# Output stage of a hybrid step: one half of the prompt tile moved behind the last pair, loads in a fixed order, and conversions tied behind gates

## The chip, the cores and the metric

The kernel runs on one core of a Trainium2 chip. The metric is the device time of one execution in microseconds, as the median of several runs. The engines of the core work from separate instruction lists, each in its own order: PE multiplies matrices into PSUM banks, ACT (ScalarE), DVE (VectorE) and POOL (GpSimd) work element by element, and SP (SyncE) issues most of the DMAs. POOL and ACT issue the others.

## The reference

One layer is computed for 128 prompt tokens and 2048 sample tokens of width 1024. A modulated RMSNorm is followed by one wide input projection; three branches (a gated delta rule, a spatial gating unit and a Fourier mixing) each give 512 columns. What matters here is the end:

```python
pb = jnp.einsum('btnw,nwd->btnd', br, w_branch)
gt = jax.nn.sigmoid(gates.reshape(B, T, N_BRANCH, D_MODEL))
merged = jnp.einsum('btnd,btnd->btd', gt, pb)
return jnp.einsum('btd,de->bte', merged, w_out), s_f, s_b
...
h = h + gate * out
y_prompt = rmsnorm(h, final_g)
```

The same last two lines, with the other group's gate, give `y_sample`.

## The kernel before

**Operands.** Each float32 operand of a product is split into a scaled float16 high part and low part, and a product is three matmuls (high by high, high by low, low by high). Weights are split on the chip: `converting` (line 289) squares a loaded block on ACT (line 305) to find its size, works out a power of two, and then writes the high part on ACT (line 317) and the low part on DVE (line 318). The loaded block waits in one of two buffers `wst`.

**Merges.** `merge` (line 1683) runs once for each branch, in the order 1, 2, 0. For each of eight blocks of output columns (`db`) and each of five token groups (four of 512 tokens, one of the 128 prompt tokens) it runs one unit: a projection of the normalized tokens `xh`, `xl` for the gate (24 matmuls), its sigmoid on ACT into `sg` (line 1714), a projection of the branch's output `o16` (12 matmuls; tile name `big`), the product of both on DVE (line 1723) and the running sum on POOL (line 1724). Both projections take their PSUM bank from a pool of three (`ps_mm`); the gate's bank is free once the sigmoid has read it. While one branch's last column block runs, `branch_block` (line 1672) loads the next branch's output into `st` and splits it into `o16` (lines 1678 and 1679). In the last merge (branch 0) the token groups run in the order 1024, 1536, prompt, 0, 512, and from column block 4 on `quarters` (line 1851) takes the finished block and the one four before it, makes the seven operand sums of a Strassen product in `T7` (two buffers), splits them (`as_pair`, lines 1809 and 1810) and writes them to the DRAM tile `pa` by a DMA that POOL issues (line 1865).

**Output.** The output projection is done in pairs of token tiles: `two_tiles` (line 1987) makes a 256-token by 1024 result from seven products of 12 matmuls of 512 columns, 84 in place of 96. The stationary operand comes from `pa` (one load of 1792 KB for a pair), the moving one from the split output weights `wohi`, `wolo`, or from sums of their quarters, which lie in DRAM as `tw` and are loaded once (four loads of 1024 KB, line 1941). The gate vector is multiplied in, the row of x added, and the row normalized (`rows_done`, line 1952). The prompt's tile is done apart and in full, by `one_tile` (line 1959): two halves of 24 matmuls, with the operands `p16` that the last merge left. Before the change it runs first, ahead of the eight pairs `firsts = [8, 10, 12, 14, 0, 2, 4, 6]`. The last pair ends by pieces, so that little is left after its last matmul: its last product is cut into 384 and 128 columns.

**Space.** The rows of x and the results lie in `room`, which is the place of `xh`; `tw` lies in the place of `xl`. A load into such a place waits only for the matmuls that still read those bytes. The pool `opa`, with two buffers of pair operands, lies where `o16` was, so a load into it waits until the last matmul of the last merge. A third buffer lies in the pool `orp`.

**What sets the order.** The program is traced in the order of the source, and a planner then gives each engine its list: it plays the program against estimated costs and takes what is ready, by priority. `tc.high_priority()` raises the priority of a block. `with tc.issue_after(x)` forbids that an instruction in the block stands ahead of `x` in the list of the same engine; it adds no wait for x's result. `gated_[0]` is the newest sigmoid traced. Each engine runs its list strictly in order, so an instruction that waits holds up all that stand behind it. The DMAs that SP issues run through one queue.

Of the kernel before, what the change touches and what calls it, by code (L numbers as in the profile page):

```python
# [188 lines left out]
def hybrid_flow_kernel(ctx: ExitStack, tc: tile.TileContext, x_prompt, x_sample, state_delta, c, c_ctx, w_ada,  # L189
# [48 lines left out]
    newest = [None]  # L238
# [55 lines left out]
    def converting(w, st, nkt, cols=P, hi=None, lo=None, tag="w", bufs=5, nth=0):  # L294
# [10 lines left out]
        w.squared = A.activation(w.lo, st, AF.Square, accum_out=ss)  # L305
# [1366 lines left out]
    def branch_block(n, s, t0, tn):  # L1672

        for g in range(4):
            st = sb(ep, [P, tn], "st", bufs=3)
            SY.dma_start(st, obD[n][g, :, t0:t0 + tn])
            yield
            A.activation(o16[:, 0, g, t0:t0 + tn], st, AF.Copy, scale=s)  # L1678
            V.scalar_tensor_tensor(o16[:, 1, g, t0:t0 + tn], st, s, o16[:, 0, g, t0:t0 + tn], ALU.mult, ALU.subtract)  # L1679

    gated_ = [None]
# [126 lines left out]
    def as_pair(hi, lo, src, s):  # L1808
        A.activation(hi, src, AF.Copy, scale=s)
        V.scalar_tensor_tensor(lo, src, s, hi, ALU.mult, ALU.subtract)  # L1810

# [38 lines left out]
    def quarters(k, t0, m4, mr):  # L1850
# [10 lines left out]
        as_pair(T7[:, :, 0, 0], T7[:, :, 1, 0], x4[:, :, 0], ms_s)  # L1861
        as_pair(T7[:, :, 0, 1:3], T7[:, :, 1, 1:3], x8, ms_s)
# [22 lines left out]
    p16, gp = [], []  # L1885
# [7 lines left out]
    def ahead_out(h0):  # L1893
        if h0:
# [3 lines left out]
            for i in range(2):  # L1898
                gp.append(sb(ep, [P, 512], "sg", bufs=4))
                SY.dma_start(gp[i], gateD[1:2, i * 512:(i + 1) * 512].to_broadcast([P, 512]))  # L1900
                scale_gate(gp[i], gp[i], winv[:, 4 * i:4 * i + 4])
            gp.append(sb(wp, [P, D], "wst", bufs=2))
            SY.dma_start(gp[2], gateD[0:1, :].to_broadcast([P, D]))
            scale_gate(gp[2], gp[2], winv)
# [20 lines left out]
    opa = pool(ctx, "opa", 2)  # L1925
    op = pool(ctx, "op", 2)
    room = xh.rearrange("p k t -> p (k t)").bitcast(F32)
    tw = xl.rearrange("p k t -> p (k t)")[:, 0:16 * D].rearrange("p (q j l k c) -> p q j l k c", q=4, j=4, l=2, k=4)
    firsts = [8, 10, 12, 14, 0, 2, 4, 6]
    ready = []  # L1930
    gb, fg = gp[2], sb(op, [P, D], "fg", bufs=1)

    def next_pair():
        i = len(ready)
        if i < len(firsts):
            ready.append(operands(orp, 1) if i % 3 == 2 else operands(opa, 2))
            SY.dma_start(ready[i].rearrange("p k l n c -> p k (l n c)"), paD[firsts[i] // 2].rearrange("k p x -> p k x"))

    next_pair()
    for q in (1, 2, 0, 3):  # L1940
        SY.dma_start(tw[:, q].rearrange("p j l k c -> p j (l k c)"), tD[q])
    SY.dma_start(fg, final_g[None, :].to_broadcast([P, D]))
    nth = [0]

    def two_rows(t, n):
        nth[0] ^= 1
        xr, hh = [[room[:, (4 * i + 2 * nth[0] + j) * D:(4 * i + 2 * nth[0] + j + 1) * D] for j in range(2)] for i in range(2)]
        for j in range(n):
            SY.dma_start(xr[j], xrows((t + j) * P, P))
        return xr, hh  # L1950

    def rows_done(t, hh, xr):
# [4 lines left out]
        SY.dma_start(y_sample[0, t * P:(t + 1) * P] if t < 16 else y_prompt[0], hh)  # L1957

    def one_tile(t, prepared, xr, hh):
        mh, ml = prepared  # L1960
        for i in range(2):
            cs = slice(i * 512, (i + 1) * 512)
            ps = bank(ps_mm, [P, 512])
            gemm_N(ps, mh, ml, wo, i * 512, 512)
            with tc.high_priority():
                V.tensor_tensor(gp[i], ps, gp[i], ALU.mult)
            G.tensor_tensor(hh[:, cs], gp[i], xr[:, cs], ALU.add)
        rows_done(t, hh, xr)
# [12 lines left out]
    def summed(q):  # L1981
        return lambda l, k: tw[:, q, :, l, k, :]

    odd_pair = [0]

    def two_tiles(t, pa, xr, hh, end):
# [5 lines left out]
        left, right = slice(0, 512), slice(512, D)  # L1992
# [19 lines left out]
        (V if end else G).tensor_tensor(hh[0][:, left], hh[0][:, left], xr[0][:, left], ALU.add)  # L2012
# [15 lines left out]
        parts = [sb(op, [P, 3], f"part{j}", bufs=1) for j in range(2)]  # L2028
        hf = [room[:, (6 - 2 * nth[0] + j) * D:(7 - 2 * nth[0] + j) * D] for j in range(2)]

        def piece(j, i, cs, on):
# [81 lines left out]
```

## Time and profile before

| | us |
|---|---|
| median of 3 runs | 2173.16 |
| lowest and highest | 2171.73, 2174.27 |
| the profiled execution | 2164.11 |
| its span | 2162.3 |
| PE busy, of the span | 2083.1 |
| granted TensorE clock, mean over the span | 0.992 |

The profile is of one execution. Times in its views are microseconds from the start of the span. A row of the timeline gives start, duration, engine, line, operation, output and inputs, and in brackets the idle time before it with what ended that. The view by windows gives the busy time of each engine in a stretch, then the granted TensorE clock as a share of full speed, the share of the DMA engines in use and GB/s. `SPq` and `POOLq` are the sequencers that issue DMAs.

### The profile page before, as it was taken

Reading aid. Unit: us, or ns where it says so; the run is one execution under the profiler, and the core shown is the slowest. Engines: PE = TensorE matmul, PEld = TensorE weight load, DVE = VectorE, ACT = ScalarE, POOL = GpSimd, SP = SyncE. Lnnn points to the kernel's source line nnn. Section 1 sums busy time; section 2 is a strip of 40 time slices with the busy share of each in tenths; the row PEclk is TensorE's granted clock in tenths of the full one; section 3 lists DMA queues with packets and bytes.
Section 4 is the critical chain, followed back from the end, with each engine's and each line's share of the span. In section 5 each row is a group of like instructions: output and inputs, shape, how many; then the busy total and the mean of one; then the engine's idle time right before and its main releaser. Section 6 shows DMA issues by size and latency. Waiting matters only on the chain.

```text
span 2162.3 us, 42634 instructions
## 1 busy us (share of the span) xinstructions
PE 2083.1 (96%) x16121; PEld 1193.1 (55%) x16121; DVE 1371.2 (63%) x3100; ACT 1062.1 (49%) x2453; POOL 753.1 (35%) x933
## 2 busy tenths in 40 slices
PE   7999999999899999899899999999999999998997
PEld 4455444456455677787565565556555444444443
DVE  6656854389778797466655546766564565565345
ACT  5554744476555663445544446655553444443111
POOL 0321432233333332443322233345443243333454
PEclk9999999999999999999999999999999999999999
DMA  9526732277776743443755556867654554556652
GB/s 351 218 77 197 256 122 81 83 232 219 243 227 223 234 148 92 132 148 112 232 170 171 164 168 184 266 204 228 210 183 163 166 185 157 182 201 263 245 217 104
DMA packets 222766, 403.24 MB, mean 186 GB/s; under 512 B 39704, under 2 KB 109744, under 8 KB 219744
## 3 DMA queue, kind: packets, MB, share of 16 engines
q1 hardware_dynamic: 167520, 290.58, 42.2%
q0 software_dynamic: 15216, 65.89, 8.1%
q10 hardware_dynamic: 39824, 44.05, 6.1%
q8 instruction: 126, 2.06, 0.4%
q14 instruction: 80, 0.66, 0.1%
HBM read 258.19 MB, written 142.24 MB: 185 GB/s over the span
## 4 chain that ended last, share of the span: by engine, by line
PE 45%; DVE 7%; DMA 6%; issue 2%; ACT 2%; POOL 1%; SPq 0%; POOLq 0%; DVEq 0%; ACTq 0%
PE b L241 44%; DMA st<-br 2%; DMA pa<-pa 1%; DMA wst<-in_w_ada_dram 1%; DVE XB L1103 1%; DVE E L1104 1%; DMA ei<-XB 1%; DVE big L1679 0%; DVE wlo L318 0%; DMA N<-n 0%; ACT big L1678 0%; POOL o L1359 0%; DVE S L1332 0%; DVE sg L466 0%; DVE o L1237 0%
## 5 line engine op out<-in xcount | busy, mean ns | idle before, releaser
L241 PE MATMUL b<-xh,whi 128*128 128x512 f16 (+1 forms) x1920 | 649.7, 347 | 3.3 <-DVE sg L1443 2.4
L241 PE MATMUL b<-xl,whi 128*128 128x512 f16 (+1 forms) x1920 | 649.9, 347 | 0.0
L241 PE MATMUL b<-xh,wlo 128*128 128x512 f16 (+1 forms) x1920 | 649.0, 347 | 0.0
L241 PEld LDWEIGHTS <-whi 128*128 128x128 f16 x3872 | 352.5, 98 | 327.6 <-issue 13.1
L241 PEld LDWEIGHTS <-wlo 128*128 128x128 f16 x1936 | 189.5, 98 | 177.6 <-issue 2.4
L241 PE MATMUL b<-big,bhi 128*128 128x512 f16 (+1 forms) x960 | 252.4, 348 | 5.0 <-ACT sg L1714 3.0
L241 PE MATMUL b<-big,blo 128*128 128x512 f16 (+1 forms) x480 | 163.6, 348 | 0.0
L1724 POOL TENSOR_TENSOR mrow<-mrow,sg 128x512 f32<-128x512 f32 (+1 forms) x80 | 93.1, 1168 | 149.1 <-DVE sg L1723 94.2
L241 PEld LDWEIGHTS <-xh 128*128 128x128 f16 x1496 | 117.2, 98 | 31.9 <-DVE yT L1629 2.6
L241 PEld LDWEIGHTS <-bhi 128*128 128x128 f16 x960 | 87.3, 98 | 78.0 <-issue 4.1
L943 POOL TENSOR_TENSOR cy<-cy,raw 128x545 f32<-128x545 f32 (+1 forms) x48 | 66.3, 1409 | 182.7 <-ACT raw L942 182.7
L1714 ACT ACTIVATE sg<-b,winv 128x512 f32<-128x512 f32 (+1 forms) x120 | 73.9, 616 | 96.0 <-PE b L241 95.2
L241 PEld LDWEIGHTS <-pa 128*128 128x128 f16 x684 | 67.0, 99 | 86.1 <-issue 8.8
L241 PE MATMUL b<-whi,xh 128*128 128x128 f16 x544 | 92.9, 219 | 3.2 <-DVE yT L1629 2.4
L1723 DVE SCALAR_TENSOR_TENSOR sg<-b,binv,sg 128x512 f32<-128x512 f32 (+1 forms) x80 | 53.4, 667 | 62.5 <-PE b L241 58.3
L241 PE MATMUL b<-whi,xl 128*128 128x128 f16 x544 | 92.9, 219 | 0.0
L241 PE MATMUL b<-wlo,xh 128*128 128x128 f16 x544 | 92.9, 219 | 0.0
L241 PE MATMUL b<-xl,pa 128*128 128x512 f16 x384 | 86.8, 379 | 0.0
L1177 POOL COPY T<-ES 32x256 f16<-32x256 f16 x68 | 30.5, 448 | 161.4 <-DMA ES<-ei 150.9
L318 DVE SCALAR_TENSOR_TENSOR wlo<-wst,wsc,whi 128x1024 f16<-128x1024 f32 x52 | 68.1, 1311 | 28.0 <-ACT whi L317 26.6
L317 ACT ACTIVATE whi<-wst,wsc 128x1024 f16<-128x1024 f32 x52 | 59.5, 1145 | 49.5 <-DVE wsc L269 47.5
L1284 POOL TENSOR_TENSOR skn<-skn,ed 128x512 f32<-128x512 f32 x34 | 38.9, 1146 | 128.0 <-DMA skn<-kv 123.0
(510 smaller groups left out, 4302.8 us busy)
## 6 DMA issues: line engine op xcount, KB each, us to landing
wst<-in_w_blk_dram SPq DMA_DIRECT2D x58, 512.0 KB, 4.1
pa<-pa POOLq DMA_DIRECT2D x16, 896.0 KB, 4.4
pa<-pa SPq DMA_DIRECT2D x8, 1792.0 KB, 8.4
qkv<-cy POOLq DMA_DIRECT2D x12, 1089.0 KB, 5.3
st<-br SPq DMA_DIRECT2D x48, 256.0 KB, 3.8
mrow<-mrg SPq DMA_DIRECT2D x16, 576.0 KB, 3.9
dc<-dec SPq DMA_DIRECT2D x17, 512.0 KB, 4.4
kq<-qkv SPq DMA_DIRECT2D x34, 256.0 KB, 5.6
```

What stands on the lines that cost most here:

```text
L241: newest[0] = PE.matmul(out, l, r, start=start, stop=stop, skip_group_check=reopened)
L317: w.made = A.activation(w.hi, st, AF.Copy, scale=s)
L318: w.low = V.scalar_tensor_tensor(w.lo, st, s, w.hi, ALU.mult, ALU.subtract)
L943: G.tensor_tensor(y[:, c0:c1], y[:, c0:c1], raw[:, 1 + c0:1 + c1], ALU.mult)
L1103: V.tensor_tensor(t3, X3[:, 0:k, k:k + 1].to_broadcast([P, k, n_]), E3[:, k:k + 1, k:32].to_broadcast([P, k, n_]), ALU.mult)
L1104: V.tensor_tensor(E3[:, 0:k, k:32], E3[:, 0:k, k:32], t3, ALU.subtract)
L1177: G.tensor_copy(T16[rows(a0, b), :, :, b], ES[0:32, :, 2 * a0 + b, :, wT])
L1284: G.tensor_tensor(h3(kn_), h3(kn_), bc(ed[:, d, t, :], P), ALU.mult)
L1714: gated_[0] = A.activation(sg, ps, AF.Sigmoid, scale=gw.inv)
L1723: V.scalar_tensor_tensor(sg, ps, binv[:, 1:2], sg, ALU.mult, ALU.mult)
L1724: G.tensor_tensor(mr, mr, sg, ALU.add)
```

## The change

The prompt tile's left half of 512 columns is still computed ahead of the pairs (`prompt_left`), without its normalization; the right half runs behind the last pair (`prompt_right`), in pieces of 384 and 128 columns, and the row is normalized there. The last pair's final product is no longer cut, and its results are scaled in place. The x row's left half has a place of its own, as have the right half and the right half of the prompt's gate vector, which POOL scales after the fourth pair; POOL then also multiplies the left half by `final_g`.

The first pair's operands are loaded into the place of `xl` (`own`), and two of the four `tw` blocks move into the pool `opa`, which keeps one buffer of pair operands. The loads at the start of the output are issued by SP in one fixed order: left half of the prompt's x, first pair's operands, `tw` 1, two rows of x, `tw` 2, `tw` 0, `tw` 3, `final_g`, the right halves of gate and x, second pair's operands, two rows, third pair's operands.

In the merges the squaring of a weight block and the high part of a branch's output may not stand ahead of the newest sigmoid traced, and in `quarters` the conversion of the block of four columns earlier comes behind that of the newest block.

```diff
+    def behind_gate():
+        return tc.issue_after(gated_[0].ins) if gated_[0] is not None else ExitStack()
...
-        w.squared = A.activation(w.lo, st, AF.Square, accum_out=ss)
+        with behind_gate():
+            w.squared = A.activation(w.lo, st, AF.Square, accum_out=ss)
...
-            A.activation(o16[:, 0, g, t0:t0 + tn], st, AF.Copy, scale=s)
+            with behind_gate():
+                A.activation(o16[:, 0, g, t0:t0 + tn], st, AF.Copy, scale=s)
...
-        as_pair(T7[:, :, 0, 0], T7[:, :, 1, 0], x4[:, :, 0], ms_s)
-        as_pair(T7[:, :, 0, 1:3], T7[:, :, 1, 1:3], x8, ms_s)
+        made = as_pair(T7[:, :, 0, 1:3], T7[:, :, 1, 1:3], x8, ms_s)
+        with tc.issue_after(made.ins):
+            as_pair(T7[:, :, 0, 0], T7[:, :, 1, 0], x4[:, :, 0], ms_s)
...
-            for i in range(2):
-                gp.append(sb(ep, [P, 512], "sg", bufs=4))
-                SY.dma_start(gp[i], gateD[1:2, i * 512:(i + 1) * 512].to_broadcast([P, 512]))
-                scale_gate(gp[i], gp[i], winv[:, 4 * i:4 * i + 4])
+            gp.append(sb(ep, [P, 512], "sg", bufs=4))
+            last_load.append(SY.dma_start(gp[0], gateD[1:2, 0:512].to_broadcast([P, 512])))
+            scale_gate(gp[0], gp[0], winv[:, 0:4])
...
-    opa = pool(ctx, "opa", 2)
+    opa = pool(ctx, "opa", 1)
...
+    own = free[:, 0:56 * P].rearrange("p (k l n c) -> p k l n c", k=4, l=2, n=7)
...
+    def in_turn(dst, src):
+        with tc.issue_after(last_load[0].ins):
+            last_load[0] = SY.dma_start(dst, src)
...
-            ready.append(operands(orp, 1) if i % 3 == 2 else operands(opa, 2))
+            ready.append(own if i % 3 == 0 else operands(opa if i % 3 == 1 else orp, 1))
...
+    tw03 = sb(opa, [P, 2, 4, 2, 4, P], "tw03", F16)
+    tw[0], tw[3] = tw03[:, 0], tw03[:, 1]
...
+        Z = bank(ps_mm, [P, 512])
+        product(Z, pa, 6, quarter(4, 512), True)
+        with tc.high_priority():
+            made = gate_add(hh[0][:, right], Z, gb[:, right], u2)
+            piece(0, 1, xr[0], hh[0], right, V)
...
+        for j in (1, 0):
+            G.tensor_tensor(norms[:, j:j + 1], parts[j][:, 1:2], mhalf, ALU.pow)
+            A.activation(hh[j], hh[j], AF.Copy, scale=norms[:, j:j + 1])
+            SY.dma_start(y_sample[0, (t + j) * P:(t + j + 1) * P], hh[j])
...
+    def prompt_left():
+        ps = bank(ps_mm, [P, 512])
+        gemm_N(ps, *p16, wo, 0, 512)
+        with tc.high_priority():
+            V.tensor_tensor(gp[0], ps, gp[0], ALU.mult)
+        G.tensor_tensor(x_left, gp[0], x_left, ALU.add)
+        A.activation(gp[0], x_left, AF.Square, accum_out=parts[2][:, 0:1])
+
+    def prompt_right():
+        after = None
+        for i, cs in ((1, slice(0, 384)), (2, slice(384, 512))):
+            ps = bank(ps_mm, [P, cs.stop - cs.start])
+            gemm_N(ps, *p16, wo, 512 + cs.start, cs.stop - cs.start)
+            with tc.high_priority(), tc.issue_after(after.ins) if i > 1 else ExitStack():
+                after = gate_add(gp_right[:, cs], ps, gp_right[:, cs], x_right[:, cs])
+                A.activation(x_right[:, cs], gp_right[:, cs], AF.Square, accum_out=parts[2][:, i:i + 1])
+                (G if i == 1 else V).tensor_tensor(gp_right[:, cs], gp_right[:, cs], fg[:, 512 + cs.start:512 + cs.stop], ALU.mult)
+        with tc.issue_after(after.ins):
+            for i in range(3):
+                summed_up(2, i)
+        n_ = norms[:, 2:3]
+        G.tensor_tensor(n_, parts[2][:, 2:3], mhalf, ALU.pow)
+        A.activation(x_left, x_left, AF.Copy, scale=n_)
+        A.dma_start(y_prompt[0, :, left], x_left)
+        V.tensor_scalar(gp_right, gp_right, n_, None, ALU.mult)
+        SY.dma_start(y_prompt[0, :, right], gp_right)
+
+    in_turn(x_left, xp_[0:P, left])
+    next_pair(in_turn)
+    sums_of(1)
+    ahead_rows = two_rows(firsts[0], in_turn)
+    sums_of(2)
+    sums_of(0)
+    sums_of(3)
+    in_turn(fg, final_g[None, :].to_broadcast([P, D]))
+    in_turn(gp_right, gateD[1:2, right].to_broadcast([P, 512]))
+    in_turn(x_right, xp_[0:P, right])
+    next_pair(in_turn)
+    prompt_left()
```

129 lines of the change are left out of this document (57 added, 72 removed).

## The prediction

> **What bounds the kernel now.** I read the page first, then the busy time by stage, the waits, and the timelines around the three places where PE stands still.
>
> ```profile
> span 2162.3 us, 42634 instructions
> PE 2083.1 (96%) x16121; PEld 1193.1 (55%) x16121; DVE 1371.2 (63%) x3100; ACT 1062.1 (49%) x2453; POOL 753.1 (35%) x933
> PE 45%; DVE 7%; DMA 6%; issue 2%; ACT 2%; POOL 1%; SPq 0%; POOLq 0%; DVEq 0%; ACTq 0%
> ```
>
> PE is busy for 96% of the span, and the change neither adds nor drops a matmul column: the last pair's 12 products of 384+128 columns become 12 of 512, and the prompt's 24 of 512 become 24 of 384+128. So it can gain only where PE stands still or has ended. The windows show where that is in the output stage (after the window: PE, PEld, DVE, ACT, POOL busy with counts, granted clock, DMA share, GB/s):
>
> ```profile
> 1981.95:1987.10 5.15, 5.15 (x25) 2.35 (x24) 1.24 (x4) 1.12 (x2) 0.00 (x0) 1.00 1.03 429
> 1987.10:1990.16 3.06, 0.19 (x2) 0.00 (x1) 2.21 (x5) 1.91 (x3) 0.00 (x0) 0.92 1.01 420
> 1990.16:1996.80 6.64, 6.64 (x24) 2.55 (x23) 3.39 (x8) 2.06 (x3) 2.67 (x3) 0.78 1.00 420
> 1996.80:2002.22 5.42, 0.13 (x1) 0.03 (x1) 1.94 (x4) 0.94 (x1) 3.66 (x3) 0.79 1.02 420
> 2002.22:2007.00 4.78, 4.78 (x12) 1.68 (x13) 1.44 (x2) 0.21 (x2) 0.57 (x1) 0.53 1.02 420
> 2007.00:2134.10 127.10, 127.10 (x590) 57.64 (x589) 49.42 (x65) 18.45 (x32) 63.08 (x57) 1.00 0.54 202
> 2144.30:2149.70 5.40, 5.37 (x37) 3.00 (x35) 5.40 (x9) 0.00 (x0) 1.34 (x1) 1.00 0.29 117
> 2149.70:2162.30 12.60, 0.00 (x0) 0.00 (x0) 6.58 (x17) 3.61 (x9) 3.70 (x4) 0.65 0.22 85
> ```
>
> The first and third rows are the prompt's halves. A full-speed 512-column matmul takes 127.10/590 = 0.215 us, 24 take 5.17. The second half took 6.64, so 1.5 went to a clock of 0.78. Before it PE stood 3.0, behind it 5.4. The first 12 matmuls of the pairs took 4.78 in place of 2.6, at a clock of 0.53: 2.2. In all 3.0 + 1.5 + 5.4 + 2.2 = **12.1 us** at the start. In the pairs themselves PE never waits, so nothing is to be had there. After the last matmul **12.6 us** pass.
>
> Who PE waited for, and why:
>
> ```profile
> PE b L241 <- DMA pa<-pa: 5.3, 1, 5.3
> PE b L241 <- ACT sg L1714: 2.9, 1, 2.9
> 1974.17 0.67 ACT L1714 ACTIVATE sg<-b,winv 128x512 f32<-128x512 f32 x1
> 1985.29 0.51 ACT L1809 ACTIVATE pa<-st,msc 128x256 f16<-128x256 f32 x1 [10.45 <-issue]
> 1989.44 0.67 ACT L1714 ACTIVATE sg<-b,winv 128x512 f32<-128x512 f32 x1
> 1974.18 0.38 PE L241 MATMUL b<-xh,whi 128*128 128x512 f16 x1
> 1982.14 19.95 DMA pa<-pa
> ```
>
> The last unit's gate product starts at 1974.18 and ends 24 matmuls later, at 1979.4. Its sigmoid ran only at 1989.44, and held the bank that the prompt's second half needed. ACT had stood 10.45 us before `pa<-st`: that is the conversion of the block four columns earlier, planned ahead of the sigmoid. The row names no cause; the other `T7` buffer's DMA, still under way, is the likely one. The 5.3 us is the first pair's load, issued at 1982.14 behind eight other loads in SP's queue, 19.95 us to landing (last row, from the chain).
>
> The same figure stands at the change from merge 2 to merge 0:
>
> ```profile
> 1708.73 0.72 ACT L1678 ACTIVATE big<-st,bsc 128x512 f16<-128x512 f32 x1 [1.73 <-DMA st<-br]
> 1709.36 0.67 ACT L1714 ACTIVATE sg<-b,winv 128x512 f32<-128x512 f32 x1
> 1710.08 0.37 PE L241 MATMUL b<-big,bhi 128*128 128x128 f16 x2 [3.01 <-ACT sg L1714]
> ```
>
> ACT waited for a branch block's load, the sigmoid stood behind its conversion, and PE lost 3.0 us.
>
> **The change part by part.**
>
> *Gates in the merges.* Two kinds of instruction may no longer be planned ahead of the newest sigmoid:
>
> ```profile
> L305 ACT ACTIVATE wlo<-wst x22: 1041/1057/1058, 1049.4 to 1897.3; 128x1024 f16<-128x1024 f32 x22
> L305 ACT ACTIVATE blo<-wst x22: 613/629/631, 1082.5 to 1915.6; 128x512 f16<-128x512 f32 x22
> L1678 ACT ACTIVATE big<-st,bsc x60: 384/721/723, 1040.6 to 1719.8; 128x512 f16<-128x512 f32 x48, 128x128 f16<-128x128 f32 x12
> ```
>
> These 44 squares and 60 conversions keep their work; only their place moves. At 1709 the sigmoid no longer stands behind the conversion: +3.0, and about 0.5, an estimate, for a lowered clock behind that stall, as behind the two of the windows: **3.5 us**. What the edge queues up: behind a waiting square stand all later ACT instructions, behind a late conversion the `st` slot, SP's next load and the weight loads behind that. The cover is time: a column block has 4 x 36 matmuls of 0.215 us plus the prompt's, 33 us, and its two weights need one square, one scale and one split each, some 1 us per step on ACT. Bounds: +5 (ACT's other waits go too) to -23 (24 column blocks, 1.06 us each, one square of the row exposed per block). I take +3.5, since in merge 0 PE shows no wait for weights that a delay would lengthen.
>
> *Order in `quarters`.* The conversion `pa<-st` goes behind its own block's newest one, so the last sigmoid has nothing unready ahead of it and can run at 1979.4. The bank is free before the prompt's left half ends. That takes 3.0 + 1.5 of the 12.1. The same 0.51 us instruction moves; what is late next is the last block's own DMA, which only pairs from the fifth on read.
>
> *First loads.* The left half of x needs the prompt unit's bytes alone, so it goes ahead. The first pair's operands go into `xl`'s first 14336 bytes, read until the fourth of eight steps of the last gate product: 1974.18 + 12 x 0.215 = 1976.8, 5.4 us before the 1982.14 of now, and they are second in the queue. PE needs them at 1981.95 + 5.17 = 1987.1. The loads and what they share the engines with:
>
> ```profile
> 1976.00:1980.00 4.00, 4.00 (x20) 1.77 (x19) 0.00 (x0) 0.00 (x0) 2.10 (x3) 1.00 0.96 274
> 1980.00:1985.00 5.00, 5.00 (x25) 2.28 (x24) 0.00 (x0) 0.00 (x0) 0.00 (x0) 1.00 0.97 389
> pa<-pa SPq DMA_DIRECT2D x8, 1792.0 KB, 8.4
> pa<-pa POOLq DMA_DIRECT2D x7, 896.0 KB, 8.0
> xl<-tw SPq DMA_DIRECT2D x4, 1024.0 KB, 16.9
> q0 software_dynamic: 114, 0.82, 64.6%
> q1 hardware_dynamic: 132, 0.47, 38.5%
> ```
>
> From 1978 to 1980 at 274 GB/s 0.55 MB come, until 1985 at 389 another 1.95, then 0.42 MB per us. The first 1.84 MB are in at 1983.3, or 1985.7 if a write of POOL's lies in between: in time. `tw` 3 is the seventh MB: 1.84 + 1.05 x 5 = 7.1 MB, and the last two blocks' writes of POOL, 0.92 each, fall into the same stretch: 8.9 MB, in at 1985 + 6.4/0.42 = 2000.3. It is needed after five products, at 1987.1 + 5 x 2.59 = 2000.1. The second pair's operands come after 2.9 MB more (`final_g`, two right halves, themselves), at 2007.2, needed at 2005.2. So PE waits about 2 us there and 0.5 in the pair. I take **2.5 us** of new waits; bounds 0 (POOL's writes fall elsewhere) and 9 (the slow 274 GB/s holds until 1985, and both waits cool the clock). The start then gains 12.1 - 2.5 = **9.6 us**.
>
> The last two rows (3 us of DMA from 2003) show why POOL's writes are in that sum: its queue takes 64.6% of the engines while both have work. Were they kept behind SP's loads, the second pair would not wait and the sum would be 2.5 us better.
>
> The windows show a clock of 0.78 behind a stand of 3.06 us; no row shows one behind 2 us. The Trainium skill, "TensorE: Matmul & The Clock Gate", Part 1 ("The HAM clock gate"), puts the fall after an idle window of some 3.4 us; by it the new waits cost no clock and the sum stays. The trace does not bear out that figure, and if 2 us cool the clock as 3.06 did, the sum is 1.5 us worse.
>
> ```profile
> 1969.06 2.03 POOL L1882 TENSOR_TENSOR sg<-sg,winv 128x512 f32<-128x512 f32 x2
> L1997 POOL TENSOR_TENSOR xh<-xh,wst 128x512 f32<-128x512 f32 x19 | 24.1, 1268 | 40.8 <-DVE xh L2002 40.8
> ```
>
> Hidden: the `scale_gate` of 512 columns (1.0 us) and the multiply (1.3) on POOL after the fourth pair (POOL is busy 63 of 127 us there), one x row and one gate load less ahead, two more behind; the store of 512 KB becomes two of 256 on two queues. If POOL's cover were gone, 2.3 us.
>
> *End.* Half the prompt's matmuls, 5.17 us, now run behind the last pair. They were in the start's sum as work, so they cost nothing by themselves; what counts is the time after the last matmul.
>
> ```profile
> 2144.29 0.33 PE L241 MATMUL b<-wohi,pa 128*128 128x384 f16 x1
> 2149.45 0.22 PE L241 MATMUL b<-wohi,pa 128*128 128x128 f16 x1
> 2153.79 1.05 DVE L2044 TENSOR_TENSOR xh<-xh,st 128x128 f32<-128x128 f32 x1
> 2154.87 0.31 ACT L2032 ACTIVATE xh<-xh 128x128 f32<-128x128 f32 x1 [0.67 <-DVE xh L2044]
> 2155.83 0.55 POOL L2066 TENSOR_TENSOR norms<-part,mhalf 128x1 f32<-128x1 f32 x1
> 2155.90 1.15 ACT L2067 ACTIVATE xh<-xh,norms 128x1024 f32<-128x1024 f32 x1 [0.62 <-POOL norms L2065]
> ```
>
> PE ends at 2149.7, but DVE is full from 2144.3 (5.40 of 5.40 us) and reaches the last piece only at 2153.79: 4 us of backlog. From the power on POOL at 2155.83 to the end of the span 6.5 us go to scaling, issue and landing. After the change PE has 2.59 + 2.59 + 5.17 = 10.35 us behind 2144.29's place. DVE's share of the pair (9.5 us until 2153.79) and one more multiply (0.7) fill 10.2 of these, then come the prompt's two gate pieces, 1.0 + 0.6 us. So the last piece ends about 1.7 us after PE; square and sums 1.0, then the 6.5: 9.2 us in place of 12.6, **3.4 us**. Bounds: 4.5 (no backlog: 8.1) and -1 (ACT's two scalings of 1024 columns, 1.15 each, and both in-place multiplies that wait for a square add 4.4).
>
> **Sum.** 9.6 + 3.5 + 3.4 = 16.5 us against the execution of 2164.11 us (span 2162.3 and 1.8 around it): 2147.6. That execution lies 9.05 under the median of the runs, 2173.16; I carry the difference over: 2173.16 - 16.5 = **2156.7 us**.
>
> **The rivals.**
>
> *Loads still late.* If the first pair's load takes its 19.95 us from 1976.8 too, it lands at 1996.8. The pairs then start 5.4 us earlier than now, but with 5.17 us of prompt still to do, and at the low clock: the start gains the 0.2 and perhaps the 1.5 of the second half. Sum 1.7 + 3.5 + 3.4 = 8.6, 2164.6. For it: the loads' own 274 GB/s at first. Against: most of the 19.95 is queueing behind 5 MB.
>
> *Planner puts something else ahead.* Both sigmoids stay late: the first pair's first bank is the one that the last sigmoid holds. Lost are 3.5 and 4.5: gain 8.5, 2164.7. Against: the edges forbid exactly what the rows show.
>
> *The end does not shrink.* In-place scaling makes DVE wait for ACT, the tail stays 12.6 or grows by 1: gain 12 to 13, about 2160.5.
>
> *Slower: weights late behind the gates.* One mechanism, in the merges: each square waits for a sigmoid, the slot `wst` comes free later, the next load and split too, and PE waits at each of 24 column blocks. It decides from 16.5/24 = 0.7 us per block; at the 1.06 us of an exposed square it costs 25, so 2156.7 + 25 = 2182. For it: ACT is strictly in order and weights have only two load buffers. Against: the 33 us per block.
>
> **How the numbers follow.** About 0.2%, 4.3 us, is what a measurement of this kernel can tell from no change. Forecast 0.55 (its own range 2150 to 2162, from the bounds of the new waits and the end); loads late 0.15, of which 0.05 end within 0.2%; planner 0.08; end 0.08, of which 0.01 within; slower 0.14. So faster 0.80, same 0.06, slower 0.14. The range leaves out the slower case and the worst late loads: 2149 to 2170.
>
> **What would show it.** Right: the first pair starts near 1983.5 on the old scale (3.5 us earlier by the merges) at a clock near 1, no wait of PE for `sg` at the end of merges 2 and 0, the first `pa` load landing before PE needs it, and about 9 us behind the last matmul. Wrong: PE waits for `tw` or `pa` beyond 4 us, waits for `bhi` or `whi` inside the merges, or DVE and ACT still working on the last pair 3 us after the last matmul.

## The result, and the profile after

The changed kernel takes 2161.59 us (median of 9 runs, 2156.92 to 2167.37) and the kernel before 2172.89 (9 runs, 2170.88 to 2176.31): ratio 0.9948, 95% interval 0.9935 to 0.996, a gain of 11.3 us. The forecast was 2156.7, so the sign and the size held, with 5 us less gain than the sum.

The two profiled executions do not show this gain: the span was 2162.3 us before and is 2164.4 now. A single profile can't be set against another by its span here, since parts of the program that the change does not touch vary by some 10 us between executions of any of these kernels (shown below). So the reading goes by stage. Head of the page of the changed kernel, then PE's waits from 1940 us on (total us, times, longest):

```profile
span 2164.4 us, 42587 instructions
PE 2088.8 (97%) x16133; PEld 1197.1 (55%) x16133; DVE 1357.1 (63%) x3101; ACT 1061.7 (49%) x2457; POOL 751.7 (35%) x933
```

```profile
PE b L244 <- DMA pa<-pa: 3.3, 1, 3.3
PE b L244 <- DMA tw<-tw: 1.0, 1, 1.0
```

The 2.9 us for the sigmoid and the 5.3 us for the first pair's operands are gone; waits for other loads have come. The view by windows of the changed kernel, from the start of the output to the end (columns as before: PE, PEld, DVE, ACT, POOL busy with counts, granted clock, DMA share, GB/s):

```profile
1993.20:1998.42 5.22, 5.22 (x25) 2.35 (x24) 3.04 (x7) 1.92 (x4) 2.25 (x3) 1.00 1.01 373
1998.42:2008.57 10.15, 10.15 (x49) 4.61 (x47) 3.35 (x5) 1.73 (x4) 3.66 (x3) 1.00 1.02 427
2008.57:2009.97 1.40, 0.38 (x2) 0.00 (x0) 0.69 (x1) 0.00 (x0) 0.00 (x0) 1.00 1.05 440
2009.97:2017.73 7.76, 7.74 (x36) 3.36 (x36) 1.39 (x2) 0.00 (x0) 3.86 (x4) 1.00 1.01 361
2017.73:2021.43 3.70, 0.38 (x2) 0.00 (x1) 0.85 (x2) 1.15 (x2) 3.62 (x3) 1.00 1.03 416
2021.43:2024.10 2.67, 2.67 (x8) 1.00 (x9) 1.35 (x2) 1.15 (x2) 1.17 (x3) 0.63 1.02 415
2145.00:2155.46 10.46, 10.44 (x73) 5.91 (x70) 10.36 (x20) 2.63 (x7) 2.84 (x4) 1.00 0.15 58
2155.46:2164.40 8.94, 0.00 (x0) 0.00 (x0) 2.28 (x8) 3.13 (x7) 1.54 (x2) 0.68 0.45 176
```

The prompt's left half takes 5.22 us and the first pair follows at once, at full clock. From start to start PE then loses 1.2 us to a wait for a block of `tw` (third row) and 3.5 us to one for the second pair's operands (fifth), and it runs behind that at a clock of 0.63. After the last matmul 8.9 us pass, where it was 12.6.

A loss stands in a stage where the prediction's sum has none, the merge of branch 2. One row of the windows for the kernel before, then the changed kernel:

```profile
1480.00:1690.00 210.00, 209.38 (x1667) 119.38 (x1665) 121.72 (x304) 106.15 (x292) 84.30 (x96) 1.00 0.61 192
```

```profile
1480.00:1690.00 210.00, 200.82 (x1627) 115.85 (x1624) 116.22 (x299) 104.02 (x299) 86.08 (x98) 0.98 0.58 182
```

PE was busy in all but 0.6 of these 210 us, and now stands 9.2.

The table below carries the experiments. Median and ratio come from the timed runs; each ratio is to the kernel before as it ran on the same chip beside the others of its group (medians 2170.59 to 2172.89), so medians of different groups can be compared to about 2 us only. The other columns are worked out from the start times of the matmuls in each trace: what lies between the starts of two successive matmuls beyond 0.2155 us per 512 columns, summed over a stretch. "Start" is the first 45 us of the output, "end" the time behind the last matmul, the other columns are stretches of the time scale (2: merge 2; 2 to 0: the change of merge; early: a stretch that no edit touches). The last five columns are of one profiled execution each, which need not be a typical one: that of blocks_gated took 2150.29 us and was its fastest.

| kernel | median us | ratio (95%) | start | end | 2: 1480–1690 | 2 to 0: 1690–1740 | early: 500–1000 |
|---|---|---|---|---|---|---|---|
| before | 2172.89 | | 12.2 | 12.7 | 6.7 | 5.6 | 50.4 |
| before_again | one run, 2174.98 | | 11.9 | 12.7 | 8.0 | 5.8 | 56.6 |
| after | 2161.59 | 0.9948 (0.9935–0.9960) | 6.6 | 8.9 | 20.1 | 2.7 | 51.4 |
| after_again | one run, 2163.9 | | 7.7 | 8.9 | 15.5 | 2.1 | 55.0 |
| no_gates | 2159.30 | 0.9938 (0.9913–0.9962) | 5.0 | 8.9 | 7.0 | 6.9 | 55.6 |
| gates_only | 2174.63 | 1.0015 (0.9999–1.0031) | 11.6 | 12.6 | 14.5 | 1.8 | 55.1 |
| squares_gated | 2152.23 | 0.9916 (0.9898–0.9935) | 6.6 | 8.9 | 7.4 | 1.0 | 57.7 |
| blocks_gated | 2159.83 | 0.9940 (0.9923–0.9958) | 4.9 | 8.9 | 7.7 | 5.0 | 50.7 |
| row_behind | 2153.60 | 0.9916 (0.9896–0.9935) | 4.2 | 8.9 | 7.4 | 1.8 | 57.9 |
| no_order | one run, 2165.43 | | 5.3 | 9.1 | 16.8 | 2.4 | 57.6 |
| pair_first | 2161.60 | 0.9955 (0.9938–0.9972) | 1.4 | 8.9 | 15.4 | 2.1 | 60.3 |
| right_ahead | 2155.01 | 0.9927 (0.9915–0.9938) | 0.1 | 11.1 | 17.2 | 5.3 | 54.2 |
| squares_pair | 2149.81 | 0.9894 (0.9874–0.9913) | 1.9 | 8.9 | 10.7 | 1.5 | 52.2 |
| squares_pair_tail | 2150.82 | 0.9894 (0.9871–0.9917) | 2.0 | 7.9 | 11.7 | 1.0 | 57.7 |

### The profile page after: what moved, and what is told of

Its sections match the earlier page's. It is cut to its first block, busy times and chain, and to the rows that moved or that the text cites. A ratio compares the mean times of both kernels' runs of the same rounds, so it can differ in the third digit from the quotient of the medians.

```text
span 2164.4 us, 42587 instructions
## 1 busy us (share of the span) xinstructions
PE 2088.8 (97%) x16133; PEld 1197.1 (55%) x16133; DVE 1357.1 (63%) x3101; ACT 1061.7 (49%) x2457; POOL 751.7 (35%) x933
## 4 chain that ended last, share of the span: by engine, by line
PE 47%; DMA 8%; DVE 5%; ACT 2%; issue 1%; POOL 1%; SPq 0%; POOLq 0%; DVEq 0%; ACTq 0%
PE b L244 47%; DMA st<-br 2%; DMA pa<-pa 1%; DMA ES<-ei 1%; DMA br<-o 1%; DMA xh<-in_x_sample_dram 1%; DMA ei<-XB 1%; DVE big L1684 1%; DMA mrg<-mrow 0%; DMA S<-in_state_delta_dram 0%; DMA skn<-kv 0%; ACT big L1683 0%; PE b L1373 0%; DMA sn<-n 0%; DVE sg L470 0%
## 5 line engine op out<-in xcount | busy, mean ns | idle before, releaser
L244 PEld LDWEIGHTS <-whi 128*128 128x128 f16 x3888 | 355.6, 98 | 328.4 <-issue 11.8
L244 PEld LDWEIGHTS <-xl 128*128 128x128 f16 x1068 | 99.0, 99 | 44.6 <-DMA tw<-tw 2.0
L321 ACT ACTIVATE whi<-wst,wsc 128x1024 f16<-128x1024 f32 x52 | 59.4, 1145 | 51.4 <-DVE wsc L272 49.5
L244 PEld LDWEIGHTS <-pa 128*128 128x128 f16 x420 | 41.4, 99 | 54.5 <-DMA pa<-pa 3.8
```

The costliest lines, as they stand in the source:

```text
L244: newest[0] = PE.matmul(out, l, r, start=start, stop=stop, skip_group_check=reopened)
L321: w.made = A.activation(w.hi, st, AF.Copy, scale=s)
```

## The experiments

### Both kernels looked at again

Both kernels unchanged, one profiled execution each: which of the differences between the first two profiles come out again?

> The kernel before, unchanged, profiled once more, to learn how far two profiles of one kernel differ and in which stage. The first pair of profiles has the changed kernel at a span 2.1 us longer than the one before, while the medians have it 11.3 us shorter. Theory 1 (the difference lies in the scan inside merges 1 and 2, which varies from run to run): this profile again loses 12.2 us of PE time at the start of the output and spends 12.6 us behind the last matmul, each within 0.5, and differs from the first profile by several us between 1000 and 1700 us. Theory 2 (the gates really slow merge 2 by 13 us, and the medians gain it elsewhere): between 1500 and 1700 us PE again loses about 6 us in excess of its matmuls, as in the first profile.

> The changed kernel, unchanged, profiled once more. Theory 1 (the scan varies): at the start of the output PE loses 6.7 us within 1, behind the last matmul pass 9.0 us within 0.5, and the loss between 1500 and 1700 us differs from the first profile's 19.5 us by 4 us or more. Theory 2 (the gates slow merge 2): that loss is 19.5 us within 2 again.

Start, end and merge 2 come out again (12 against 7 to 8, 12.7 against 8.9, 8 against 15.5). The span of the kernel before was 2173.2 in this execution, 10.9 more than in the first; 6.2 of that lie in the stretch from 500 to 1000. So the spans of one pair of executions say nothing about 10 us, and the stages do.

### The gates against the rest of the change

no_gates takes the two edges in the merges out of the changed kernel, gates_only puts them alone into the kernel before.

```diff
-        with behind_gate():
-            w.squared = A.activation(w.lo, st, AF.Square, accum_out=ss)
+        w.squared = A.activation(w.lo, st, AF.Square, accum_out=ss)
...
-            with behind_gate():
-                A.activation(o16[:, 0, g, t0:t0 + tn], st, AF.Copy, scale=s)
+            A.activation(o16[:, 0, g, t0:t0 + tn], st, AF.Copy, scale=s)
```

> The changed kernel without the two gates in the merges: squares and branch conversions may again stand ahead of the newest sigmoid. The prediction's theory (the gates take 3.5 us at the change from merge 2 to merge 0; the traces made it 2.7): the ratio to the kernel before is 0.9960 to 0.9965, against 0.9948 for the whole change, and PE waits 3 us for a sigmoid at the end of merge 2 again. Rival (the gates delay the scan's neighbours in merge 2 and cost several us): without them the kernel is faster than the changed one, ratio 0.991 or less.

> The kernel before with the two gates in the merges alone. The prediction's theory: 2.7 to 3.5 us faster than the kernel before, ratio 0.9984 to 0.9988, with the start of the output and the end as before (12.2 us lost, 12.6 us behind the last matmul). Rival (the gates cost in merge 2): slower, ratio 1.002 or more. If the ratio is 1.000 within 0.001, the gates do nothing that can be measured.

Without the gates the change gains 13.5 us by its ratio; the gates alone give 1.0015 (0.9999 to 1.0031). They do what they were predicted to do at 1709 (5.6 to 5.8 us lost there become 1.8), and cost 6.5 to 7.8 us in merge 2 of gates_only, 7.5 to 13.4 in the two profiles of the changed kernel. The wait is not for weights, and little of it is the clock: 0.99 over the stretch in gates_only, 0.98 in the changed kernel, which is 1.7 and 3.4 us. PE's longest waits of gates_only between 1480 and 1690:

```profile
PE b L244 <- ACT o L1234: 5.9, 3, 4.3
PE b L244 <- DVE o L1375: 0.2, 1, 0.2
```

`o` at line 1234 is the scan's output block, which runs between the merge's units. ACT stands at it because the block's buffer is still being stored. SP's queue, ACT and PE in gates_only, in order:

```profile
1582.31 0.38 SPq L1263 DMA_DIRECT2D skn<-kv  x1
1589.86 0.32 SPq L1701 DMA_DIRECT2D mrow<-mrg  x1
1590.27 0.38 SPq L1261 DMA_DIRECT2D sk<-kT  x1
1590.76 0.37 SPq L1377 DMA_DIRECT2D br<-o  x1
...
1595.62 1.14 ACT L1234 ACTIVATE o<-b,eg 128x128 f32<-128x128 f32 x4 [7.83 <-DMA br<-o]
...
1596.82 1.44 PE L244 MATMUL b<-u,sqk 128*128 128x128 f16 x12 [4.25 <-ACT o L1234]
```

SP stands 7 us at the load of a row of sums (`mrow`, line 1701), whose buffer is not free; the store `br<-o` is queued behind it; ACT waits 7.83 us for the store, PE 4.25 us for ACT. Over the 210 us ACT stands 21.3 us for these stores here and 19.9 in the changed kernel, but 7.3 in no_gates. In SP's list the order of these two kinds is (s the store of line 1377, M the load of line 1701):

```
before, and every kernel with one gate or none:  s s s M s M s M s M s M s M s M s M ...
every kernel with both gates, row_behind aside:  s s s M s M M s s M s M s M M s s M M s s M M ...
```

The edges are on ACT alone; that SP's list changes is the planner's doing, which plays all engines against its estimates. It also changes the order on ACT, DVE and POOL there.

### Which gate

In squares_gated only the squaring of weight blocks is kept behind the sigmoid, in blocks_gated only the branch block's conversion.

```diff
squares_gated:
-            with behind_gate():
-                A.activation(o16[:, 0, g, t0:t0 + tn], st, AF.Copy, scale=s)
+            A.activation(o16[:, 0, g, t0:t0 + tn], st, AF.Copy, scale=s)
blocks_gated:
-        with behind_gate():
-            w.squared = A.activation(w.lo, st, AF.Square, accum_out=ss)
+        w.squared = A.activation(w.lo, st, AF.Square, accum_out=ss)
```

> The changed kernel with the gate on the squares alone. Theory A: from 1480 to 1700 us PE loses 14 us or more, SP stands at the load of the running sum ahead of the scan's store of its output, ACT waits for that store, and from 1700 to 1800 the loss is 7 us as without gates: ratio 0.9965, the worst of all variants with the new output stage. Theory C: the loss in merge 2 is 7 to 8 us as without gates.

> The changed kernel with the gate on the branch conversions alone; squares go free. The traces with both gates lose 14.6 to 20.1 us of PE time from 1480 to 1700 us, those without 6.7 to 8.0, while the 100 us from 1700 lose 2.6 to 3.7 with gates and 7.1 to 8.1 without. Theory A (the squares' gate reorders the scan's neighbours in merge 2; the conversions' gate brings the gain at the change to merge 0): both stretches at their low value, ratio to the kernel before about 0.992, better than the 0.9938 without gates. Theory B (either gate alters the plan enough): 1480 to 1700 loses 14 us or more again, ratio 0.995. Theory C (the conversions' gate itself delays the scan): this one loses in merge 2 and the next one does not.

Each alone leaves merge 2 as it was (7.4 and 7.7, one profile each). The gate on the squares alone takes away the loss at the change of merge almost in full (1.0); the one on the conversion, which is the instruction that the prediction saw in the sigmoid's way, leaves 5.0. A gate forbids a place ahead of the newest sigmoid traced, not behind the one that comes next, and with blocks_gated PE still waits there, now for the product behind the sigmoid:

```profile
PE b L244 <- DVE sg L1725: 2.5, 1, 2.5
```

Why the squares' gate puts the sigmoid first is the planner's choice again, and was not followed further.

### The order on SP's queue

row_behind keeps both gates and forbids the load of `mrow` in merge 2 a place ahead of the scan's newest store.

```diff
-        SY.dma_start(obD[0][:, :, t * P:(t + 1) * P].rearrange("h p t -> p h t"), h3(o))
+        stored_[0] = SY.dma_start(obD[0][:, :, t * P:(t + 1) * P].rearrange("h p t -> p h t"), h3(o))
...
-                    SY.dma_start(mrow, mD[db][:, h0:h0 + hn])
+                    with tc.issue_after(stored_[0].ins) if stored_[0] is not None and n == 2 else ExitStack():
+                        SY.dma_start(mrow, mD[db][:, h0:h0 + hn])
```

> The changed kernel with both gates kept; in merge 2 the load of the row of sums (mrow from mrg) may not be queued on SP ahead of the newest store of the scan's output (br from o) traced. Theory (the two gates together put the load ahead of the store on SP's queue, and what costs time is the store that stands behind it, not the gates): the loss of PE between 1480 and 1690 us falls from the 20.1 and 15.5 us of the two profiles of the changed kernel to the 7 to 8 of the kernels with one gate or none, PE no longer waits for the scan's product o, the other stages stay, and the median comes to 2149 to 2154, ratio about 0.990. Rival (the gates hold ACT up themselves, and the order on SP is only a sign of it): the loss stays at 14 or more, and the median within 3 us of the changed kernel's 2161.6.

2153.6 us, as the theory had it. Store and load stand next to each other in SP's queue again, the store first, ACT's stand for the store shrinks, and PE is busy in the whole stretch (row_behind: SP, ACT, then the window):

```profile
1586.52 0.37 SPq L1377 DMA_DIRECT2D br<-o  x1
1586.98 0.46 SPq L1702 DMA_DIRECT2D mrow<-mrg  x1
1590.66 1.14 ACT L1234 ACTIVATE o<-b,eg 128x128 f32<-128x128 f32 x4 [1.72 <-DMA br<-o]
```

```profile
1480.00:1690.00 210.00, 209.45 (x1713) 121.27 (x1711) 120.67 (x306) 106.33 (x306) 91.47 (x103) 1.00 0.61 197
```

So merge 2 loses no more with both gates than without them (7.4 against 7.0) once the store goes first. The medians of the changed kernel and of row_behind lie 8.0 us apart (2161.59 - 2153.60), on two chips; by the ratios it is 7.0, with intervals that touch at 0.9935. The one new edge is on SP's queue, but the planner moves some entries of the other lists with it, POOL's and DVE's more than ACT's, so that the queue's order is the cause with this much left open.

### The order in `quarters`

no_order is the changed kernel with the conversion of the block of four columns earlier first again.

```diff
-        made = as_pair(T7[:, :, 0, 1:3], T7[:, :, 1, 1:3], x8, ms_s)
-        with tc.issue_after(made.ins):
-            as_pair(T7[:, :, 0, 0], T7[:, :, 1, 0], x4[:, :, 0], ms_s)
+        as_pair(T7[:, :, 0, 0], T7[:, :, 1, 0], x4[:, :, 0], ms_s)
+        as_pair(T7[:, :, 0, 1:3], T7[:, :, 1, 1:3], x8, ms_s)
```

> The changed kernel with the quarters' conversions in the old order (the block of four columns earlier first). Theory (this order alone took the last sigmoid out from behind the conversion): ACT's last sigmoid is late again, PE waits 3 to 4 us for the product of the last gate before the output starts, and the loss of the first 45 us of the output goes from 6.6 and 7.7 us to 9 to 12; the end stays at 8.9. Rival (the gates in the merges have already taken the conversion out of the way): the last sigmoid is in time and the loss stays at 6.5 to 8.

My theory fell, and so did the rival: gates_only has the gates, the old order in `quarters` and the old loads, and there PE still loses 2.9 us to the last sigmoid. In no_order the start loses 5.3 us, 1.3 below the changed kernel, and 1.5 more are lost in the last units ahead of it (4.1 against 2.6, from the same start times): no difference in sum that one profile could tell. The conversion stands 4.86 us where it stood 10.45 before. What it waits for can be read now: POOL's write of the other `T7` buffer. The timeline (issue) and the view of DMA issues (KB, us to landing) of the kernel before, then the same of no_order with the conversion's row:

```profile
1975.40 0.75 POOL L1865 DMA_DIRECT2D pa<-pa  x1 [4.31 <-DVE pa L1810]
```

```profile
pa<-pa POOLq DMA_DIRECT2D x1, 896.0 KB, 9.8
```

```profile
1985.95 0.75 POOL L1869 DMA_DIRECT2D pa<-pa  x1 [4.38 <-DVE pa L1813]
1990.25 0.51 ACT L1812 ACTIVATE pa<-st,msc 128x256 f16<-128x256 f32 x1 [4.86 <-issue]
```

```profile
pa<-pa POOLq DMA_DIRECT2D x1, 896.0 KB, 4.2
```

1975.40 + 9.8 = 1985.2, and the conversion of the kernel before ran at 1985.29; 1985.95 + 4.2 = 1990.15, and here it ran at 1990.25. So the conversion waited for this write, as supposed. But the write was late while it shared the DMA engines with SP's eight loads, issued from 1975.02 to 1979.7; the records show its first packet at about 1980.7, five us behind the issue, against one us in no_order. In the fixed order the second load, the first pair's, may start only when `xl`'s place is read, and holds SP until then (1988.48 here); the write runs alone and lands in 4.2 us. With the new order of the loads the last sigmoid is in time, and the order of the conversions on top adds nothing that can be seen. Whether the conversions' order would do it alone, with the old loads, was not tried.

### The loads at the start

pair_first moves the second pair's load ahead of `final_g` and the right halves, which nothing needs before the first pair's end; right_ahead computes the prompt's right half ahead of the pairs again, with the new loads, and normalizes the prompt's row after the fourth pair (the diff shows the calls only).

```diff
pair_first:
-    in_turn(fg, final_g[None, :].to_broadcast([P, D]))
-    in_turn(gp_right, gateD[1:2, right].to_broadcast([P, 512]))
-    in_turn(x_right, xp_[0:P, right])
     next_pair(in_turn)
+    in_turn(fg, final_g[None, :].to_broadcast([P, D]))
...
+            in_turn(gp_right, gateD[1:2, right].to_broadcast([P, 512]))
+            in_turn(x_right, xp_[0:P, right])
right_ahead:
...
+    in_turn(gp_right, gateD[1:2, right].to_broadcast([P, 512]))
+    in_turn(x_right, xp_[0:P, right])
...
     prompt_left()
+    prompt_right()
...
-    prompt_right()
```

> The changed kernel with the second pair's operands loaded ahead of the final gain, and the right halves of gate and x behind the third pair's operands. In the changed kernel the second pair waited 3.3 us, its first 9 matmuls ran at a low clock (1.9 us), and the three small loads ahead of its operands took about 3.6 us of the queue, of which the two right halves 2.4 at half the usual rate. Theory 1 (the order alone makes that wait): the operands land 3 to 4 us earlier, the second pair waits under 0.5 us with no low clock, 4 to 5 us faster than the whole change, ratio 0.9925 to 0.9930. Theory 2 (the volume until the second pair binds, since POOL's writes share the engines): the wait falls by under 1.5 us, ratio 0.994 or worse.

> The changed kernel with the right half's 24 matmuls ahead of the pairs again, behind the left half's; its two loads come right behind the first pair's operands, and the prompt's normalization runs after the fourth pair. Theory 1 (the new waits at the start come from too little PE work over the loads): 5.17 us more work over the same loads take most of the 6.7 us lost at the start, at most 2.5 us stay, while the time behind the last matmul returns from 9.0 to about 12 us: ratio between 0.9930 and 0.9945, 1 to 2 us better than the whole change. Theory 2 (the start is bound by what is issued first, not by how much work lies over it): the second pair still waits 3 us or more for its operands, and the ratio is 0.996 or worse.

In the profile both take the wait for the second pair away: PE's one wait left in pair_first is 0.8 us for `tw`, and right_ahead has none, with 1.4 and 0.1 us lost at the start in place of 6.6. right_ahead pays at the end, where DVE's backlog of the last pair is back: 11.1 us in place of 8.9. So the move of the right half gains 2.2 us at the end and gives up 5.2 us of cover for the loads at the start.

The medians do not follow. pair_first gives 2161.6, no gain over the changed kernel, and right_ahead 2155.0, 6.6 below pair_first, where by the stages it should lie a few us above it. What makes that difference is open. So is what the move of the right half is worth in the time: right_ahead, which leaves it ahead of the pairs, is not slower than the changed kernel but 6.6 us faster by the medians (0.9927 against 0.9948, intervals that overlap a little). Merge 2 runs badly in both profiles, but the profiled execution of right_ahead was its slowest, 2165.0 us, with the other six at 2153.9 to 2156.95, and no profile of one of those was taken.

### Together

squares_pair joins the earlier load to the one gate on the squares (the two diffs above). squares_pair_tail also has ACT scale the last pair's second result behind the prompt's squares:

```diff
-        for j in (1, 0):
-            G.tensor_tensor(norms[:, j:j + 1], parts[j][:, 1:2], mhalf, ALU.pow)
+        def stored(j):
             A.activation(hh[j], hh[j], AF.Copy, scale=norms[:, j:j + 1])
             SY.dma_start(y_sample[0, (t + j) * P:(t + j + 1) * P], hh[j])
+        for j in (1, 0):
+            G.tensor_tensor(norms[:, j:j + 1], parts[j][:, 1:2], mhalf, ALU.pow)
+        stored(1)
+        rest.append(stored)
...
+        with tc.issue_after(squared.ins):
+            rest[0](0)
```

> The changed kernel with the gate on the weight blocks' squaring alone, and with the second pair's operands loaded ahead of final_g and the two right halves. Theory (the parts add up): loss of the first 45 us of the output about 1.4 us as with the earlier load alone, 7.5 between 1480 and 1690 and 1 between 1690 and 1740 as with the one gate alone, the end 8.9; against the 2152.23 of the one gate alone the earlier load takes up to 5 us more, so 2147 to 2152, ratio about 0.9895. Rival (the earlier load gives nothing in the time, as its own median of 2161.6 against 2161.59 would have it): 2152 to 2154, 0.9916.

> The same, and ACT scales the last pair's second result only behind the prompt tile's last squaring. Theory (ACT's 1.1 us scaling of that result stands ahead of the squaring on which the prompt's norm waits): the squaring ends about 1.2 us sooner, the end behind the last matmul goes from 8.9 to 7.6 to 8.0 us, and the median lies 1 us below the kernel without this step, ratio about 0.989. Rival (the second result's store, issued later, now ends last): the end stays within 0.3 us of 8.9 or grows, and nothing is gained.

2149.81 us, 0.9894: the lowest median of all, 11.8 us below the changed kernel, inside what the theory gave. Against squares_gated's 0.9916 the intervals overlap, so that the earlier load gains in the time is likely and not shown. Merge 2 lost more than with the one gate alone (10.7 and 11.7 against 7.4), although the lists of ACT, DVE, POOL and SP there are those of squares_gated, so this is a difference between executions. PE waits for line 1234 here too (3.8 us in squares_pair): one store was issued 1.2 us behind its product and took 5.0 us to land, where that of squares_gated was issued at once and took 3.4. Why was not found.

The last step shortens the end by 1.03 us, as priced. ACT in the changed kernel, then in squares_pair_tail (last matmul at 2155.22 and 2141.51):

```profile
2154.89 2.19 ACT L2054 ACTIVATE xh<-xh,norms 128x1024 f32<-128x1024 f32 x2 [1.22 <-POOL norms L2053]
2156.98 0.51 ACT L2092 ACTIVATE xl<-xl 128x384 f32<-128x384 f32 x1
2158.95 0.55 POOL L2098 TENSOR_TENSOR norms<-part,mhalf 128x1 f32<-128x1 f32 x1 [0.30 <-DVE part L2069]
```

```profile
2141.16 1.15 ACT L2053 ACTIVATE xh<-xh,norms 128x1024 f32<-128x1024 f32 x1 [1.22 <-POOL norms L2057]
2142.22 0.51 ACT L2098 ACTIVATE xl<-xl 128x384 f32<-128x384 f32 x1
2143.02 1.14 ACT L2053 ACTIVATE xh<-xh,norms 128x1024 f32<-128x1024 f32 x1
2144.19 0.55 POOL L2106 TENSOR_TENSOR norms<-part,mhalf 128x1 f32<-128x1 f32 x1 [0.30 <-DVE part L2073]
```

From the last matmul's start to the prompt's first square 1.76 us become 0.71. The median does not show it (2150.82, ratio 0.9894 again): 1 us is a quarter of what this kernel's measurement can tell.

## Why the prediction was right, and where it was not

**First loads: right.** The first pair's load was issued at 1988.04, 5.16 us ahead of the output's start as worked out; it took 7.4 us to land, and PE needed it 10.4 us after the issue. The rival of loads still late fell.

**New waits at the start: the mechanism was right, the size off.** The term was 2.5 us, with 2 for the second pair and 0.5 in the first. Measured are 3.5 and 1.2 (the latter for `tw` 0 behind the fourth product, not for `tw` 3 behind the fifth), and 1.7 of low clock behind the longer stand, for which the sum had nothing: 6.6 and 7.7 in the two executions, inside the bounds of 0 and 9. The sum took 0.42 MB/us for all that lies ahead of the second pair. The windows of the changed kernel show one stretch that ran at little more than half of that, while the two right halves came in:

```profile
2010.00:2013.00 3.00, 2.99 (x14) 1.20 (x15) 0.22 (x1) 0.00 (x0) 0.00 (x0) 1.00 0.98 410
2013.00:2015.00 2.00, 2.00 (x11) 0.94 (x10) 0.47 (x1) 0.00 (x0) 1.37 (x2) 1.00 1.04 237
2015.00:2018.00 3.00, 3.00 (x15) 1.20 (x13) 0.69 (x1) 0.00 (x0) 2.75 (x3) 1.00 1.02 402
```

The engines are full throughout. At 237 in place of 420 GB/s these 2 us bring 0.37 MB less, which delays the second pair by 0.9 us. These two loads have rows of 2048 bytes for each partition, the others 3584 and more, but the length of the rows is not shown to be the reason: in row_behind a packet of 2048 bytes took 88 ns in mean from 2001 to 2003, here 175 from 2013 to 2014 and 130 in the next us, and before the change a stretch of loads with rows of 4096 and 8192 bytes ran at 274 GB/s. What slows such stretches is open.

So the start gained 4 to 6 us in place of 9.6 in the changed kernel's two profiles, and 7 to 8 in no_gates, blocks_gated, row_behind and no_order. What sets these apart is the clock, not the gates: in those four it stayed at full speed behind the stand for the second pair, 2.7 to 3.7 us long, and in the two of the changed kernel it fell behind 3.5 and 3.9 us, for 1.7 and 2.6 us of loss (last section). Without that loss all six lie between 4.2 and 5.3 us.

**Order in `quarters`: right effect, wrong cause.** The last sigmoid ran 1.7 us ahead of the output's start, where the step had it 2.5 ahead. But no_order shows that with the new loads the old order has it in time too.

**End: right.** 8.93 us against 9.2 predicted, gain 3.7 against 3.4. The parts differ: DVE ended 0.7 us behind PE, not 1.7, and ACT's two scalings then held up the prompt's square, which the sum had put in its lower bound only.

**Gates in the merges: the step that failed.** "I take +3.5, since in merge 0 PE shows no wait for weights that a delay would lengthen." The 3.5 at 1709 came (5.6 to 5.8 us lost there, then 2.1 to 2.7), though a wait for `sg` was to be gone there and PE still shows 1.1 to 1.8 us for the product behind the sigmoid. But merge 2, for which the step had nothing, lost 7 to 8 us by row_behind, so the gates' net is a loss. The medians put it at about 2 us (2161.59 against 2159.30, intervals that overlap), the stages of the profiles at 4 to 9. The bound of -23 covered the size; the mechanism was not among the rivals. The one that I named, weights late behind the gates, did not occur: no PE wait for a weight block stands among the longest of merge 2. I asked what is queued behind the waiting instruction on ACT, and not what the planner does to the other queues when an edge delays one engine in its model.

**The sum.** From the two profiles of each kernel: start +4.8, end +3.7, change of merge +3.3, last units of merge 0 +1.3, merge 1 and its surroundings (1000 to 1480) +2.8, merge 2 -10.4: 5.5 us. By row_behind's median, merge 2 cost 8.0, which makes it 7.9. The median gained 11.3. The 3 to 6 us between are not located; the early stretch varies by 10 between executions, and the four profiles can't settle less. So what the stages show is a third to a half of the 16.5 that were added up. That the forecast came within 5 us is in part luck: the sum lacked the loss in merge 2 and put the start 5 too high, and gains that it did not have, most of them not located, made up for part of that.

## What to carry to other kernels

An edge that orders one engine's list can reorder the list of another when a planner makes both: before pricing such an edge, list the long waits of the in-order DMA queue in that stage and ask which stores would be stuck behind them. A load issued early can hold back what is on the other queues: price it together with the transfers already under way, and at the rates that the trace shows, which here went from 237 to 440 GB/s with the engines full. And where unchanged stages vary by 10 us, compare stages of the traces and medians of the runs, and never two spans.

## What was not expected of the hardware

**A write of POOL's behind loads of SP's.** The same 896 KB write took 4.2 us with the engines free until its last microsecond and 9.8 us with eight loads issued between 0.4 us ahead of it and 4.3 behind. The Trainium skill, "DMA: Bandwidth & Descriptors", section "Anatomy of one DMA — SWDGE (gpsimd) path", gives a line of 2.0 us plus bytes by 436 KB per us, which makes an estimate of 4.1 us for this write; the free case agrees.

**The clock behind a short stand.** After a stand of 3.5 us the next matmuls of the changed kernel ran at 0.63 (2021.43 to 2024.10), and before the change one of 3.03 us was followed by 0.78. But in no_order a stand of 3.74 us at the same place was followed by full clock (its windows, the stand and what comes behind it):

```profile
2018.27:2022.22 3.95, 0.38 (x2) 0.00 (x1) 0.85 (x2) 1.28 (x3) 3.87 (x4) 1.00 1.03 417
2022.22:2026.00 3.78, 3.78 (x18) 1.77 (x19) 2.63 (x3) 1.61 (x3) 0.93 (x2) 1.00 1.03 420
```

So the length of a stand does not decide it alone. In the clock records of all fourteen traces the clock changes only at the steps of a fixed grid of 3.41 us. What goes with a fall is how much of one step PE stands idle, counting 0.2155 us of work for 512 columns: of the steps at full clock from 30 us on, those idle for over three quarters were followed by half clock in 46 of 46 cases, those idle for less than 0.6 in none of 8,382; between, it went both ways. The 3.03 us filled 0.74 of one step, the 3.5 us 0.8, the 3.74 us of no_order 0.56 at most. The figure of the Trainium skill, "TensorE: Matmul & The Clock Gate", Part 1 ("The HAM clock gate"), an idle window of some 3.4 us, lies above the 3.03 us that were followed by a fall and below the 3.74 that were not.

**Variation of unchanged stages.** PE's loss between 500 and 1000 us ranged from 50.4 to 60.3 us over the fourteen profiles of kernels whose source is the same there. Part of it is the clock: its mean over this stretch was 1.000 in the first profile of the kernel before, 0.990 in the second and 0.986 in pair_first, which is 0, 5.1 and 6.9 us, beside losses of 50.4, 56.6 and 60.3. It is not all: right_ahead lost 6.9 us to the clock too, and 54.2 in all.
